# The last norm moved behind its transposes, and gates built for four tokens at a time

## The chip, the cores and the metric

The kernel runs on one core of one Trainium2 chip. The metric is the device time of one execution in microseconds (us). The shown runs of the kernel before took 3232.64, 3232.66 and 3237.02 us, the median is 3232.66 us. One more execution was recorded by the profiler; the profile below is of that one.

## The reference, cut to what matters

T = 256 tokens, width D = 2048, everything in fp32. Two blocks follow each other: attention and an MLP, then a recurrent mixer (HGRN2 and gated delta rule) and a layer of 16384 experts (PEER). The change touches the end of the mixer and the expert layer:

```
h  = h + mix @ w_out                                  # output projection, residual
hn = h * rsqrt(mean(h*h) + eps) * g                   # the norm ahead of the experts
q  = hn @ w_query                                     # 8 heads x 2 halves x 128
s1, s2 = q1 . sub_keys[0], q2 . sub_keys[1]           # 128 scores per half and head
v1, i1 = top_k(s1, 16); v2, i2 = top_k(s2, 16)        # then the best 16 of the 256 sums
expert = i1 * 128 + i2;  gate = softmax(best)
hid = gelu(hn @ u[e])                                 # kept where e is among the chosen
y   = sum over chosen e of gate_e * hid_e * v[e]
out = rmsnorm(h + y)
```

Chosen experts are not gathered. The kernel computes `hn @ u[e]` for all 16384 experts, multiplies the Gelu of it with a gate that is zero for experts not chosen, and multiplies the result with all of v.

## The kernel before, in words

**Products.** A weight matrix is read in pieces of 128 x 1024 (512 KB) into a tile `raw` by SP's DMA queue (line 90). ScalarE (ACT) rounds a piece to `hi` (L103), VectorE (DVE) forms the rest, `lo = raw - hi` (L104), and TensorE (PE) multiplies three times: hi with both parts of x, lo with x's first part. `wstat` (L117 to L128) holds the weights stationary: one call reads two pieces (the two halves of the contraction), runs 2 x 24 matmuls of 128 x 256 (L125) and gives 128 outputs for 256 tokens in a PSUM tile `acc`. For the expert layer there are 3 `raw`, 3 `hi` and 2 `lo` tiles. A piece's load waits on SP until its `raw` tile, used three pieces earlier, has been read by that piece's L104.

**End of the mixer.** `out_proj("w2_oa", [mixA], end_mix)` forms the last half of the output projection, 512 columns (`nb`, 0 to 3) and 128 tokens (`tt`, 0 and 1) at a time. `end_mix` adds each result to the residual x (L935), takes sums of squares on ACT, writes x to memory (`xd`), and after the last piece of a token half forms the norm's scale `r4` (a reduction and a small operation on DVE, a power on GpSimd, L247 and L248).

**The norm.** After that, x is scaled, `xs = x * r4` (L954, eight pieces of 128 x 512 on DVE). PE transposes xs in 32 pieces of 128 x 128 (L959); 16 times ACT and DVE split a transposed 128 x 256 piece into the two parts of `XT` (L114, L115). Then come the queries.

**Queries and scores.** 16 calls of `wstat` with `peer_q` give q, which ACT copies to `qT` (L1101). After each second call, eight fp32 matmuls with `sub_keys` (L1001) give the scores of a head, which ACT copies to `sc` (L1004). A generator, `topk`, works in the background on DVE from then on, into the first dozen u blocks, paced by the calls of `tick`.

**The u blocks.** 128 calls of `wstat` with `peer_u` follow. ACT applies Gelu to each result into a column block of `H` (L1150). Once the top-k is done, gates are built between the blocks by `gates` (L1104 to L1133), two tokens a call, 128 calls spread evenly up to block `G1` = 126: DVE compares a ramp with the first index of two tokens (`oh1`, L1108) and, for each token, with its second index times the gate (`oh2`, L1113), PE multiplies them (L1116), ACT copies one half of the result (L1120), DVE adds the other (L1123 or L1129) and multiplies into the columns of H that are there already (L1124, L1130, L1132); ACT copies the rest. Blocks that come after a token's gate get Gelu into `ut` (L1153) and a product on DVE (L1154).

**The v products** (L1180 to L1182) read H and end the kernel.

**What sets the order.** A scheduler arranges the instructions of the program into one list per engine; each engine takes its list strictly in order and waits on semaphores. Pieces under `tc.high_priority()` (loads, hi, lo, Gelu) are put as early as their inputs allow. Which tile an instruction may write is set by pools with a number of buffers (`bufs`).

## Time and profile before

| | |
|---|---|
| median of the runs shown | 3232.66 us |
| the profiled execution, and its span | 3235.04 us, 3233.3 us |
| TensorE busy | 3199.8 us, 99% of the span |
| VectorE busy | 2108.1 us, 65% |
| ScalarE busy | 1656.9 us, 51% |
| granted TensorE clock, mean | 0.997 of full speed |
| the norm ahead of the experts | about 1669 to 1686 us |
| queries; u blocks; v products | from 1686; from 1782; from 2516 us |
| top-k ends; gates | about 1840 us; 1883 to 2505 us |

The span is the time between the first and the last recorded instruction. A busy share is an average over the whole span: DVE is busy 90% of the time in some stages and far less in others. Rows of a timeline give the start and the duration of an instruction; an engine starts the next one a little before the last one's recorded end, so what an instruction costs in a row of instructions is the distance of starts. A matmul's recorded end is modelled; the distance of starts is what counts there too.

### The profile page before, as it was taken

How to read it: one execution, taken by the hardware profiler on the slowest of the kernel's cores; microseconds unless marked ns; L12 is line 12 of the kernel's file. 1: busy time of each engine (PE TensorE's matmuls, PEld its weight loads, DVE VectorE, ACT ScalarE, POOL GpSimd, SP SyncE). 2: the span in 40 equal slices, each digit the busy share in tenths (PEclk: the TensorE clock that was granted, in tenths of full speed). 3: DMA queues.
4: the chain of work that ended last, by engine and by line, in shares of the span. 5: the costliest groups of instructions: out<-in, count | busy, mean ns of one | idle time of the engine just before them, and what ended most of it. 6: DMA issues, size and time to landing. Idle time of an engine off the chain costs nothing.

```text
span 3233.3 us, 53579 instructions
## 1 busy us (share of the span) xinstructions
PE 3199.8 (99%) x21252; PEld 2909.6 (90%) x21252; DVE 2108.1 (65%) x3587; ACT 1656.9 (51%) x2453; POOL 25.2 (1%) x40
## 2 busy tenths in 40 slices
PE   9999999999999999999999999999999999999998
PEld 7989899899898889899889999999999888888886
DVE  4555665555555686478759867788888555555554
ACT  5447554444443564467444456655555544444444
POOL 0000000000000000000000000000000000000000
PEclk9999999999999999999999999999999999999999
DMA  6454555555555543354455555555555655555654
GB/s 226 151 169 160 186 189 195 193 191 190 190 189 194 185 138 114 111 164 141 151 182 177 177 177 184 185 184 184 184 181 185 209 190 193 191 191 192 215 190 162
DMA packets 162156, 578.71 MB, mean 179 GB/s; under 512 B 19056, under 2 KB 20720, under 8 KB 161520
## 3 DMA queue, kind: packets, MB, share of 16 engines
q1 hardware_dynamic: 156384, 565.36, 52.7%
q10 hardware_dynamic: 5520, 9.93, 0.9%
q8 instruction: 166, 2.72, 0.3%
q14 instruction: 86, 0.70, 0.1%
HBM read 571.02 MB, written 4.19 MB: 178 GB/s over the span
## 4 chain that ended last, share of the span: by engine, by line
PE 50%; DVE 2%; DMA 0%; ACT 0%; issue 0%; POOL 0%; DVEq 0%; POOLq 0%; ACTq 0%; SPq 0%
PE acc L125 23%; PE acc L1181 7%; PE acc L1180 7%; PE acc L1182 7%; PE acc L163 1%; PE acc L164 1%; PE acc L165 1%; PE misc L1116 1%; DVE lo L104 1%; PE misc L873 0%; DVE oh L1065 0%; DMA raw<-in_peer_v 0%; PE misc L1001 0%; ACT hi L103 0%; DVE es L1071 0%
## 5 line engine op out<-in xcount | busy, mean ns | idle before, releaser
L104 DVE TENSOR_TENSOR lo<-raw,hi 128x1024 fp32r<-128x1024 f32 x987 | 1206.6, 1223 | 854.5 <-ACT hi L103 497.4
L103 ACT ACTIVATE hi<-raw 128x1024 fp32r<-128x1024 f32 x1010 | 1071.0, 1061 | 1232.7 <-PE acc L164 359.4
L125 PE MATMUL acc<-xt,hi 128*128 128x256 f32 x8704 | 1522.8, 279 | 0.2 <-ACT hi L103 0.2
L125 PEld LDWEIGHTS acc<-xt,hi 128*128 128x128 f32 x8704 | 1321.4, 188 | 4.4 <-issue 3.2
L125 PE MATMUL acc<-xt,lo 128*128 128x256 f32 x4168 | 1159.0, 278 | 3.0 <-DVE lo L104 3.0
L125 PEld LDWEIGHTS acc<-xt,lo 128*128 128x128 f32 x4168 | 786.9, 189 | 4.2 <-DVE lo L104 4.2
L1181 PE MATMUL acc<-hi,xt 128*128 128x512 f32 x1024 | 402.7, 393 | 0.2 <-DVE xt L112 0.2
L1182 PE MATMUL acc<-lo,xt 128*128 128x512 f32 x1024 | 399.1, 390 | 1.6 <-DVE lo L104 1.6
L1180 PE MATMUL acc<-hi,xt 128*128 128x512 f32 x1024 | 400.3, 391 | 0.0
L1182 PEld LDWEIGHTS acc<-lo,xt 128*128 128x128 f32 x1024 | 192.2, 188 | 44.8 <-DVE lo L104 3.3
L1180 PEld LDWEIGHTS acc<-hi,xt 128*128 128x128 f32 x1024 | 192.2, 188 | 44.4 <-ACT hi L103 0.3
L1181 PEld LDWEIGHTS acc<-hi,xt 128*128 128x128 f32 x1024 | 192.4, 188 | 40.7 <-DVE xt L112 0.6
L164 PE MATMUL acc<-hi,act 128*128 128x512 f32 x512 | 199.5, 390 | 0.0
L165 PE MATMUL acc<-lo,act 128*128 128x512 f32 x512 | 199.5, 390 | 0.0
L163 PE MATMUL acc<-hi,act 128*128 128x512 f32 x512 | 199.2, 389 | 0.0
L163 PE MATMUL acc<-hi,xt 128*128 128x512 f32 x384 | 155.9, 406 | 2.1 <-ACT hi L103 2.1
L164 PE MATMUL acc<-hi,xt 128*128 128x512 f32 x384 | 151.4, 394 | 0.0
L165 PE MATMUL acc<-lo,xt 128*128 128x512 f32 x384 | 151.1, 394 | 0.0
L1113 DVE SCALAR_TENSOR_TENSOR oh<-c_iota,sl,slg 128x256 fp32r<-128x256 f32 x256 | 120.2, 477 | 0.0
L163 PEld LDWEIGHTS acc<-hi,act 128*128 128x128 f32 x512 | 96.1, 188 | 19.9
L164 PEld LDWEIGHTS acc<-hi,act 128*128 128x128 f32 x512 | 96.1, 188 | 19.9
L165 PEld LDWEIGHTS acc<-lo,act 128*128 128x128 f32 x512 | 96.1, 188 | 19.5
(580 smaller groups left out, 2874.9 us busy)
## 6 DMA issues: line engine op xcount, KB each, us to landing
raw<-in_peer_u SPq DMA_DIRECT2D x256, 512.0 KB, 3.6
raw<-in_peer_v SPq DMA_DIRECT2D x194, 512.0 KB, 4.3
raw<-in_w_up SPq DMA_DIRECT2D x128, 512.0 KB, 3.6
raw<-in_w_down SPq DMA_DIRECT2D x128, 512.0 KB, 3.5
raw<-in_w_qkf SPq DMA_DIRECT2D x32, 512.0 KB, 3.5
raw<-in_w_qka SPq DMA_DIRECT2D x32, 512.0 KB, 3.5
raw<-in_w_b SPq DMA_DIRECT2D x32, 512.0 KB, 3.5
raw<-in_w_fq SPq DMA_DIRECT2D x32, 512.0 KB, 3.9
```

Source lines behind the costliest of these rows:

```text
L103: S.activation(hi, r, AF.Copy)
L104: V.tensor_tensor(out=lo, in0=r, in1=hi.bitcast(F32), op=OP.subtract)
L125: PE.matmul(ps, lhsT=a[:, w], rhs=X[s][:, j, b], start=(s == 0 and j == 0 and a is hi and b == 0), stop=(s == 1 and j == 7 and a is lo))
L163: PE.matmul(ps, lhsT=x[:, 0], rhs=hi[:, w], start=(first and j == 0), stop=False)
L164: PE.matmul(ps, lhsT=x[:, 1], rhs=hi[:, w], start=False, stop=False)
L165: PE.matmul(ps, lhsT=x[:, 0], rhs=lo[:, w], start=False, stop=(last and j == 1))
L1113: V.scalar_tensor_tensor(oh2, iota[:, None].to_broadcast([128, 2, 128]), sl2[:, t:t + 1], slg.bitcast(F32)[:, t, :, None].to_broadcast([12 ...
L1116: PE.matmul(gps[:, j * 256:(j + 1) * 256], lhsT=oh1[:, j], rhs=oh2.rearrange("p a b -> p (a b)"), start=(j == 0), stop=True, skip_group_ch ...
L1180: PE.matmul(o, lhsT=x[:, 0], rhs=hi[:, w], start=first, stop=False)
L1181: PE.matmul(o, lhsT=x[:, 1], rhs=hi[:, w], start=False, stop=False)
L1182: PE.matmul(o, lhsT=x[:, 0], rhs=lo[:, w], start=False, stop=last)
```

## The change

**The norm.** x is transposed unscaled: r4 is one factor per token, and Gelu's argument, q and the scores are linear in x. `end_mix` now calls `xt_piece` (eight transposes, four splits with the gain `gcols`) as soon as columns `nb` of x are there (nb 0 to 2); the last eight transposes come in the background of the first query product, which runs on the old pools. `bcast` copies r4 along the free dimension into `r4B` (two diagonal matrices on DVE, two fp32 matmuls, an ACT copy). The scale is applied to the scores (two ACT copies with a scale per head in place of one) and to each u block: DVE forms `t = ps * r4B` (128 x 256) ahead of Gelu, which now reads `t` in SBUF. The 8 pieces of L954 are gone. mixA lies in two tiles of another pool.

**The gates.** A call of `gates` serves four tokens, 64 calls: `oh1` is one instruction of 128 x 512, `oh2` stays one per token, the sum and its copy stay one per two tokens, the products with H are one per H tile for four tokens. Buffers: `oh1` 2 to 1, `oh2` 4 to 3, `gs` 1 (it shared `ut`, 2), `ut` 2 to 1, `scr` 2 to 1.

```diff
     def end_mix(nb, tt, ps):
...
             rsqrt(r4[:, tt:tt + 1], s4[:, tt:tt + 1], 1, 1.0 / D)
-
-    out_proj("w2_oa", [mixA], end_mix)
+        elif tt == 1:
+            xt_piece(x, nb, XT, gcols[:, 4])
+
+    def end_norm():
+
+        with tc.high_priority():
+            xt_piece(x, 3, XT, gcols[:, 4])
+        yield
+        bcast(r4, r4B, xp)
+
+    out_proj("w2_oa", mixA, end_mix)
...
-    XT = new_xt()
-    nx = xq.enter_context(tc.tile_pool(name="nx", bufs=1, reuse_waits="tile"))
-    xs = [nx.tile([128, 2, 512], F32, name="xs", bufs=4) for _ in range(4)]
-    for tt in range(2):
-        for nb in range(4):
-            V.tensor_scalar(out=xs[nb][:, tt], in0=x[:, tt, nb * 512:(nb + 1) * 512], scalar1=r4[:, tt:tt + 1],
-                            scalar2=None, op0=OP.mult)
-    for c in range(16):
-        ps = misc()
-        for tt in range(2):
-            PE.transpose(ps[:, tt * 128:(tt + 1) * 128], xs[c // 4][:, tt, c % 4 * 128:(c % 4 + 1) * 128], ident)
...
+    bg.append(end_norm())
+    first_q = wstat(I["peer_q"][0], XT)
+    drain()
...
-        S.activation(sc, sps.rearrange("p (i n) -> p i n", i=4), AF.Copy)
+        for tt in range(2):
+            S.activation(sc.rearrange("p (a b) n -> p a b n", a=2)[:, :, tt],
+                         sps.rearrange("p (a b n) -> p a b n", a=2, b=2)[:, :, tt], AF.Copy, scale=r4[:, tt:tt + 1])
...
     def gates(g, c):
...
+        t0 = 4 * g
+        oh1 = pp2.tile([128, 4, 128], F32R, name="oh1", bufs=1)
+        V.tensor_tensor(out=oh1, in0=iota[:, None].to_broadcast([128, 4, 128]),
+                        in1=sl1[:, t0:t0 + 4, None].to_broadcast([128, 4, 128]), op=OP.is_equal)
+        gs = pp2.tile([128, 4, 128], F32, name="gs", bufs=1)
+        for i in range(2):
+            gps = misc()
+            for j in range(2):
+                t = t0 + 2 * i + j
+                oh2 = pp2.tile([128, 2, 128], F32R, name="oh2", bufs=3)
+                V.scalar_tensor_tensor(oh2, iota[:, None].to_broadcast([128, 2, 128]), sl2[:, t:t + 1],
...
+                PE.matmul(gps[:, j * 256:(j + 1) * 256], lhsT=oh1[:, 2 * i + j],
...
+            S.activation(gs[:, 2 * i:2 * i + 2], gv[:, :, 1], AF.Copy)
+            V.tensor_tensor(out=gs[:, 2 * i:2 * i + 2], in0=gv[:, :, 0], in1=gs[:, 2 * i:2 * i + 2], op=OP.add)
+        for i in range(2):
+            hv = H[i][:, :, t0:t0 + 4].rearrange("p b t -> p t b")
+            d = min(max(c - 64 * i, 0), 64)
             if d:
+                V.tensor_tensor(out=hv[:, :, :d], in0=gs[:, :, 64 * i:64 * i + d], in1=hv[:, :, :d], op=OP.mult)
+            if d < 64:
+                S.activation(hv[:, :, d:], gs[:, :, 64 * i + d:64 * i + 64], AF.Copy)
...
         with tc.high_priority():
+            t = pp2.tile([128, T], F32, name="ut", bufs=1)
+            V.tensor_tensor(out=t, in0=ps, in1=r4B, op=OP.mult)
             if n < T:
-                S.activation(hb[:, n:], ps[:, n:], AF.Gelu)
+                S.activation(hb[:, n:], t[:, n:], AF.Gelu)
             if n:
-                t = pp2.tile([128, T], F32, name="ut", bufs=2)
-                S.activation(t[:, :n], ps[:, :n], AF.Gelu)
+                S.activation(t[:, :n], t[:, :n], AF.Gelu)
                 V.tensor_tensor(out=hb[:, :n], in0=t[:, :n], in1=hb[:, :n], op=OP.mult)
-        while len(H) == 2 and done < 128 and b + 1 >= g0 + done * (G1 - g0) / 128:
+        while len(H) == 2 and done < 64 and b + 1 >= g0 + done * (G1 - g0) / 64:
```

The lines of the changed kernel are up to nine higher: the new product `t` is L1158, Gelu L1160 and L1162, the product with H of a block L1163; in `gates`, oh1 is L1119, oh2 L1127, the matmul L1130, the copy L1133, the sum L1134, the products with H L1139.

**Where instructions moved, first place: PE in the u blocks, around block 100.** In the kernel before, the two gate matmuls of a call stand behind the last matmul of one u block (`acc_25832`) and ahead of the first of the next (`acc_25912`):

```order
L125 MATMUL acc_25832<-xt_16306,lo_25842 128x256
L1116 MATMUL misc_25897<-oh2_25900,oh1_25898 128x256 [waits PE_49]
L1116 MATMUL misc_25897<-oh2_25903,oh1_25898 128x256
L125 MATMUL acc_25912<-xt_16305,hi_25915 128x256 [waits Activation_49]
L125 MATMUL acc_25912<-xt_16305,lo_25916 128x256 [waits DVE_49]
```

In the changed kernel three of the four gate matmuls stand there, between block 100 (`acc_25658`) and block 101 (`acc_25748`):

```order
L125 MATMUL acc_25658<-xt_15974,lo_25668 128x256
L1130 MATMUL misc_25727<-oh2_25728,oh1_25724 128x256 [waits PE_49]
L1130 MATMUL misc_25727<-oh2_25731,oh1_25724 128x256
L1130 MATMUL misc_25736<-oh2_25737,oh1_25724 128x256 [waits PE_49]
L125 MATMUL acc_25748<-xt_15973,hi_25751 128x256 [waits Activation_49]
...
L125 MATMUL acc_25748<-xt_15973,lo_25752 128x256
L1130 MATMUL misc_25736<-oh2_25740,oh1_25724 128x256 [waits DVE_49]
L125 MATMUL acc_25748<-xt_15973,hi_25751 128x256 x2
```

The fourth moved into the next block, behind 21 of its matmuls, and waits there for `oh2_25740` on DVE.

**Second place: DVE in the same stretch.** Before, with the block that ends (`ut_25814` is its Gelu), the sum and the two `oh2` of the next call, whose matmuls come a block later:

```order
L104 TENSOR_TENSOR lo_25842<-raw_25839,hi_25841 128x1024 [waits DMAHW5_49,PE_49,Activation_49]
L1108 TENSOR_TENSOR oh1_25978<-c_iota_16415,sl0_16417 128x256 [waits PE_49]
L1154 TENSOR_TENSOR H1_19031<-ut_25814,H1_19031 128x194 [waits Activation_49]
L1129 TENSOR_TENSOR ut_25826<-misc_25817,ut_25826 128x256 [waits Activation_49]
L1113 SCALAR_TENSOR_TENSOR oh2_25980<-c_iota_16415,sl1_16418,slg_16419 128x256
L1130 TENSOR_TENSOR H0_16414<-ut_25826,H0_16414 128x2x64 [waits DVE_49]
L1132 TENSOR_TENSOR H1_19031<-ut_25826,H1_19031 128x2x36
L1113 SCALAR_TENSOR_TENSOR oh2_25983<-c_iota_16415,sl1_16418,slg_16419 128x256
L104 TENSOR_TENSOR lo_25916<-raw_25913,hi_25915 128x1024 [waits DMAHW6_49,PE_49]
```

Now, from the end of block 100 (`ut_25719` is its scaled result) to the second piece of block 102:

```order
L1158 TENSOR_TENSOR ut_25719<-acc_25658,r4B_15972 128x256 [waits DVE_49,PE_49]
L104 TENSOR_TENSOR lo_25758<-raw_25755,hi_25757 128x1024 [waits DMAHW7_49,Activation_49]
L1163 TENSOR_TENSOR H1_19067<-ut_25719,H1_19067 128x196 [waits DVE_49,Activation_49]
L1134 TENSOR_TENSOR gs_25726<-misc_25727,gs_25726 128x256 [waits Activation_49]
L1127 SCALAR_TENSOR_TENSOR oh2_25740<-c_iota_16470,sl1_16473,slg_16474 128x256
...
L104 TENSOR_TENSOR lo_25818<-raw_25815,hi_25817 128x1024 [waits DMAHW0_49,PE_49]
L1134 TENSOR_TENSOR gs_25726<-misc_25736,gs_25726 128x256 [waits Activation_49]
L1119 TENSOR_TENSOR oh1_25880<-c_iota_16470,sl0_16472 128x512
L1139 TENSOR_TENSOR H0_16469<-gs_25726,H0_16469 128x4x64 [waits DVE_49]
L1139 TENSOR_TENSOR H1_19067<-gs_25726,H1_19067 128x4x37
L1158 TENSOR_TENSOR ut_25809<-acc_25748,r4B_15972 128x256 [waits PE_49]
L104 TENSOR_TENSOR lo_25824<-raw_25821,hi_25823 128x1024 [waits DMAHW1_49,Activation_49]
```

The call's last `oh2` stands behind the product with the finished block's Gelu and behind the sum; two more `oh2` of the next call stand where the dots are. On ACT, `hi_25817` (block 102) stands ahead of block 100's Gelu as the corresponding `hi` did before.

**Third place: ACT between the first and the second query product.** Before, the first piece of the second (`hi_16496`) stood ahead of the copy of the first result:

```order
L114 ACTIVATE xt_16306<-misc_16377,gcols_88 128x256 [waits PE_49]
L103 ACTIVATE hi_16496<-raw_16494 128x1024 [waits DMAHW6_49]
L114 ACTIVATE xt_16306<-misc_16382,gcols_88 128x256 [waits PE_49]
L103 ACTIVATE hi_16502<-raw_16500 128x1024 [waits DMAHW7_49,DVE_49,PE_49]
L1101 ACTIVATE qT_16491<-acc_16430 128x256 [waits PE_49]
L103 ACTIVATE hi_16559<-raw_16557 128x1024 [waits DMAHW0_49,DVE_49,Activation_49]
```

Now:

```order
L114 ACTIVATE xt_15974<-misc_16421,gcols_88 128x256 [waits PE_49]
L947 DMA xd_15969<-x_87 256x1x512
L1112 ACTIVATE qT_16485<-acc_16369 128x256 [waits PE_49]
L278 ACTIVATE r4B_15972<-misc_16450 128x256 [waits PE_49]
L103 ACTIVATE hi_16490<-raw_16488 128x1024 [waits DMAHW6_49]
```

The first piece of the second product (`hi_16490`) now stands behind the copy of the first result and behind the copy of `r4B`.

## Rows read from the trace of the kernel before

**Rows 1.** The page: busy time, share and count of each engine.

```profile
PE 3199.8 (99%) x21252; PEld 2909.6 (90%) x21252; DVE 2108.1 (65%) x3587; ACT 1656.9 (51%) x2453; POOL 25.2 (1%) x40
```

**Rows 2.** Waits of PE over the span: line, releaser, us, times, longest.

```profile
PE misc L959 <- DVE xs L954: 3.5, 2, 3.1
...
PE misc L873 <- DVE aT L877: 2.0, 1, 2.0
```

**Rows 3.** Timeline of PE around 1670: start, duration, idle before.

```profile
1669.18 0.39 PE L165 MATMUL acc<-lo,xt 128*128 128x512 f32 x1
...
1673.69 1.11 PE L959 MATMUL misc<-ident,xs 128*128 128x128 f32 x4 [3.08 <-DVE xs L954]
```

**Rows 4.** Timeline of ACT: the copy of the first query product.

```profile
1686.06 0.39 ACT L1101 ACTIVATE qT<-acc 128x256 f32<-128x256 f32 x1 [1.54 <-PE acc L125]
```

**Rows 5.** Windows: busy time (count) of each engine, PEclk the granted clock.

```profile
1465.00:1467.00 2.00, 2.00 (x12) 2.00 (x11) 0.42 (x4) 1.99 (x3) 0.00 (x0) 0.50 0.03 10
1670.00:1675.00 5.00, 1.73 (x8) 1.08 (x8) 3.84 (x11) 1.52 (x4) 0.56 (x1) 0.70 0.37 142
1820.00:1840.00 20.00, 18.08 (x147) 17.47 (x148) 19.93 (x28) 7.04 (x9) 0.00 (x0) 1.00 0.48 159
```

**Rows 6.** Timeline of PE: eight fp32 score matmuls.

```profile
1697.17 1.05 PE L1001 MATMUL misc<-sub_keys,qT 128*128 128x128 f32 x8
```

**Rows 7.** Lines by form: a product of PSUM with a broadcast scale on DVE.

```profile
L282 DVE TENSOR_TENSOR pad<-acc,r3B 128x256 f32<-128x256 f32 x16 | 6.8, 424 | 17.6 <-PE acc L125 17.6
```

**Rows 8.** Timeline of PE: gate matmuls, each behind the end of a u block.

```profile
2456.80 0.40 PE L1116 MATMUL misc<-oh,oh 128*128 128x256 f32 x2
...
2462.50 0.40 PE L1116 MATMUL misc<-oh,oh 128*128 128x256 f32 x2
...
2468.19 0.40 PE L1116 MATMUL misc<-oh,oh 128*128 128x256 f32 x2
```

**Rows 9.** Timeline of DVE in the same stretch.

```profile
2462.75 1.23 DVE L104 TENSOR_TENSOR lo<-raw,hi 128x1024 fp32r<-128x1024 f32 x1 [0.90 <-PE acc L125]
2463.89 0.42 DVE L1108 TENSOR_TENSOR oh<-c_iota,sl 128x256 fp32r<-128x256 f32 x1
2464.80 0.41 DVE L1154 TENSOR_TENSOR H<-ut,H 128x238 f32<-128x238 f32 x1 [0.49 <-ACT ut L1153]
2465.13 0.42 DVE L1129 TENSOR_TENSOR ut<-misc,ut 128x256 f32<-128x256 f32 x1
2465.46 0.47 DVE L1113 SCALAR_TENSOR_TENSOR oh<-c_iota,sl,slg 128x256 fp32r<-128x256 f32 x1
2465.86 0.46 DVE L1130 TENSOR_TENSOR H<-ut,H 128x128 f32<-128x128 f32 x1
2466.22 0.42 DVE L1132 TENSOR_TENSOR H<-ut,H 128x110 f32<-128x110 f32 x1
2466.54 0.48 DVE L1113 SCALAR_TENSOR_TENSOR oh<-c_iota,sl,slg 128x256 fp32r<-128x256 f32 x1
...
2469.92 0.40 DVE L1154 TENSOR_TENSOR H<-ut,H 128x240 f32<-128x240 f32 x1
```

**Rows 10.** Timeline of ACT in the same stretch.

```profile
2463.38 1.06 ACT L103 ACTIVATE hi<-raw 128x1024 fp32r<-128x1024 f32 x1 [0.95 <-DMA raw<-in_peer_u]
2464.34 0.17 ACT L1150 ACTIVATE H<-acc 128x18 f32<-128x18 f32 x1
2464.41 0.36 ACT L1153 ACTIVATE ut<-acc 128x238 f32<-128x238 f32 x1
```

**Rows 11.** Tile raw, 1885 to 2505: idle before its instructions; landing times.

```profile
  DMA raw<-in_peer_u: 41.9, 33
...
DMA to landing us min/median/max: 3.0/3.6/6.1
```

**Rows 12.** Lines by form of ACT, 2300 to 2310: SBUF and PSUM sources.

```profile
L1133 ACT ACTIVATE H<-ut 128x74 f32<-128x74 f32 x1 | 0.3, 341 | 0.5 <-DVE ut L1129 0.5
...
L1150 ACT ACTIVATE H<-acc 128x84 f32<-128x84 f32 x1 | 0.2, 222 | 0.0
```

More of the change, by code (lines that the diff above doesn't have):

```diff
@@ L919, in build, with mix_a @@
     proj_tok("w2_ag", zA, AF.Silu)
-    mixA = xtp.tile([128, 8, 2, T], F32R, name="xt", bufs=2)
+    mixA = []
+    def mix_a(i):
+        while not set(range(4 + 4 * i, 8 + 4 * i)) <= made:
+            yield
+        mixA.append(hp.tile([128, 4, 2, T], F32R, name="Z", bufs=3))
+        yield from head_norm_t(oA[i], mixA[i], lambda h: hg, hp, 0, 4,
+                               z=zA[:, :, i * 512:(i + 1) * 512].rearrange("p a (h d) -> p a h d", h=4))
     for i in range(2):
-        bg.append(head_norm_t(oA[i], mixA, lambda h: hg, hp, 4 * i, 4,
-                              z=zA[:, :, i * 512:(i + 1) * 512].rearrange("p a (h d) -> p a h d", h=4),
-                              ready=lambda i=i: set(range(4 + 4 * i, 8 + 4 * i)) <= made))
+        bg.append(mix_a(i))
     for nb in range(4):
@@ L930, in build @@
     r4 = sm.tile([128, 2], F32, name="r4")
+    r4B = sm.tile([128, T], F32, name="r4B")
+    XT = new_xt()
     def end_mix(nb, tt, ps):
@@ L1094, in build @@
     for c in range(16):
-        ps = wstat(I["peer_q"][c], XT)
+        ps = wstat(I["peer_q"][c], XT) if c else first_q
         if c and c % 2 == 0:
@@ L1104, in gates @@
     def gates(g, c):
-        gps = misc()
-        oh1 = pp2.tile([128, 2, 128], F32R, name="oh1", bufs=2)
-        V.tensor_tensor(out=oh1, in0=iota[:, None].to_broadcast([128, 2, 128]),
-                        in1=sl1[:, 2 * g:2 * g + 2, None].to_broadcast([128, 2, 128]), op=OP.is_equal)
-        for j in range(2):
-            t = 2 * g + j
-            oh2 = pp2.tile([128, 2, 128], F32R, name="oh2", bufs=4)
-            V.scalar_tensor_tensor(oh2, iota[:, None].to_broadcast([128, 2, 128]), sl2[:, t:t + 1],
-                                   slg.bitcast(F32)[:, t, :, None].to_broadcast([128, 2, 128]),
-                                   op0=OP.is_equal, op1=OP.mult)
-            PE.matmul(gps[:, j * 256:(j + 1) * 256], lhsT=oh1[:, j], rhs=oh2.rearrange("p a b -> p (a b)"),
-                      start=(j == 0), stop=True, skip_group_check=True)
```

29 lines of the change are left out of this document (9 added, 20 removed).

## The prediction, made before the changed kernel ran

> **What bounds the kernel now.** I read the page first: PE is busy 99% of the span, 3199.8 us [rows 1], so time is won or lost only where PE stands still, runs at the lower clock, or gets more to do. The change adds two small fp32 matmuls and takes none away. The list of PE's waits then says where it stands still: 3.5 us ahead of the norm's transposes, and little else near the change [rows 2]. Around the gates it waits almost nowhere. Two places remain to be worked out: the norm, where something can be won, and the u blocks, where PE has no wait yet and the change hangs one of its matmuls on DVE.
>
> **The norm, before.** The last matmul of the output projection starts at 1669.18 and gives way 0.23 later; the first query product is done when ACT copies it, at 1686.06, some 0.2 after PE's last matmul [rows 3, 4]. That is 16.45 us. The 48 matmuls in it are worth 48 x 0.114 = 5.5 us (two u blocks with four gate matmuls take 2468.19 - 2456.80 = 11.39, so 0.114 each [rows 8]). The 32 transposes are fp32 with 128 columns, as the score matmuls are, of which eight end within 1.05, so about 0.1 each [rows 6], 3.2 us. The rest, 7.8 us, is lost: 3.1 in one wait for xs [rows 3], some small ones, and the lower clock behind them (0.70 granted on average from 1670 to 1675, half speed for a good part of it [rows 5]).
>
> **The norm, after.** The 24 early transposes lie between matmuls of the output projection, and the last eight in the first query product, so the long wait goes. What is late next:
> - The add of the last 512 columns stands on DVE behind the first diagonal (which waits for GpSimd's power) and a `lo`, and PE reaches those transposes first: about 0.8, and 0.4 for the transposes of nb 2, which stand right behind their adds. 1.2 together, bounds 0.5 and 3.1 (the wait of before [rows 3]).
> - Between the first and second query product ACT now does the copy of q, then r4B, then the second product's `hi` (third place of the order). From PE's last matmul: 0.2, copy 0.36, r4B 0.36, hi 0.97 (2463.38 to 2464.34 [rows 10]), lo 1.22 [rows 9] are 3.1; two matmuls run ahead of the `lo` (0.2) and two score matmuls fill 0.2 that they would cost elsewhere: 2.7. The bounds are 1.5 (the copies are short and the load stands ready) and 5 (sub_keys, now issued later on the same queue, lands late).
> - Two diagonal matmuls, of which one lies in this gap: 0.1 to 0.2.
> - A PE wait of 2.0 us earlier in the kernel [rows 2] was followed by a stretch at half speed (1465 to 1467 [rows 5]). This gap is as long; I take 3 us of half speed, which cost 1.5, bounds 0 and 3.
> The gain is 7.8 - 1.2 - 2.7 - 0.1 - 1.5 = 2.3 us, bounds about -3 and +6.
>
> **The top-k stretch.** DVE is full there (19.93 of 20 us [rows 5]) and PE waits for it in places. Each u block now has `t` on DVE as well, 0.33 each (the form of L282, 0.424 long [rows 7], with the distance of starts that the equally long sum has, 2465.13 to 2465.46 [rows 9]). Eleven blocks make 3.7 at most. As `lo` stands ahead of top-k work where it can, a part of this delays the top-k and not PE: 1.5 taken, bounds 0 and 3.7.
>
> **The u blocks with gates.** Count DVE's work first. Per four tokens the changed gates save one start of `oh1` and little else (the products with H cost per element: 0.36 for 128 elements, 0.32 for 110 [rows 9], so 0.65 for 256), about 0.2 x 64 = 13 us over the stage; `t` adds 108 x 0.33 = 36. By its share that would still fit beside PE. What does not fit is the place of the fourth gate matmul (first and second place of the order). Let F be the end of a u block. PE runs three gate matmuls and 21 of the next block, and at F + 24 x 0.114 = F + 2.73 it meets a matmul that waits for an `oh2`. On DVE this `oh2` stands behind the product with the finished block's Gelu (L1154 before, L1163 now) and the sum of the gates. In the rows that product starts at F + 1.73 in one block (2468.19 to 2469.92) and at F + 2.30 in the block ahead, where ACT's `hi` had waited 0.95 for its load, and Gelu stands behind that `hi` [rows 8, 9, 10]. From there to the end of the `oh2` it is 2464.80 to 2465.46 plus 0.47 = 1.13 [rows 9]. So it is ready at F + 2.86 or F + 3.43, and PE waits 0.13 or 0.70. In the kernel before nothing of this touches PE: both `oh2` are made a block ahead. Everything of the u block is queued behind the waiting matmul, so the time is lost for good; waits under a us, 6 to 12 us apart, should not lower the clock.
>
> How often is the load late? Before, `hi` waits for a load 33 times, 41.9 us in all [rows 11], so it has no room to spare. And now there is a closed loop, with a group every second block, late in the stage. After the awaited `oh2`, DVE does two more `oh2` (0.80), a `lo` (1.14), a sum (0.33), `oh1` of 512 (0.60: 0.33 for 256 columns plus what a `lo` costs per column), H0 (0.65), H1 at 140 elements (0.38), `oh2` (0.40), `t` (0.33) and the `lo` that frees a `raw` tile (1.22): 5.85. Then the load, 3.65 with 0.1 for its issue and signal [rows 11], `hi` 0.96, Gelu 0.07 and 0.39 [rows 10], the product 0.33, the sum 0.33, the `oh2` 0.40: 6.23. That is 12.08 for two blocks, against 11.39 on PE: 0.69 lost per group. At the end of the stage H1 has 240 elements, 0.93. Early, without H1 and with half of H0, the loop is 11.3, and what is left is the direct wait of about 0.1; with H0 whole, 0.36. Over the blocks 18 (1883 less 1782 us, at 5.7) to 126, weighted by their number (18 at 0.1, 28 at 0.2, 62 at 0.67), that is 0.45 per group, and 64 x 0.45 = 29 us. (The groups come every 1.7 blocks, not every second; where two come in adjacent blocks, DVE's list without any idle time is some 6.8 us between the two `oh2`, against 5.9 on PE, so the loss is no smaller.) Bounds: nothing, if the `oh2` is ready in time; 64 x 0.13 = 8, if loads are never late; 64 x 1.0 = 64, if loads that overlap land 0.55 later than the median on average, which the longest, 6.1 [rows 11], leaves room for. I take 29: the loop rests on rows, and both ends need something that they don't show.
>
> The source of Gelu also changes, from PSUM to SBUF. A copy from SBUF of 74 columns (in strides) takes 0.341, Gelu from PSUM of 84 columns 0.222 [rows 12]; I leave it out of the sum. [...]
>
> **Switch to the v products.** The last gates end a block earlier, and the first `lo` of v comes 0.33 later; PE needs it after that: 0.
>
> **Sum.** Against the profiled execution, 3235.04 (span 3233.3, 1.7 around it): -2.3 + 1.5 + 29 = +28.2, 3263.2. That execution is 2.4 above the median of the runs: 3260.8, so 3261.
>
> **Rivals.**
> 1. The loads keep up, and only the direct wait is left: +8 in the gates, 3240. For it: a median landing of 3.6 and many blocks in which `hi` waited for PE instead. Against: `t` and the burst of four tokens put the `lo` that frees the tile later than before. Chance 0.13.
> 2. The loads overlap more and land later, 1.0 per group: 3235.04 - 2.3 + 1.5 + 64 - 2.4 = 3296. For it: DVE's two `lo` follow each other closer in the burst. Against: at a slower pace each load has more room. Chance 0.13.
> 3. The other side: the awaited `oh2` is ready, because Gelu starts before F + 1.0 and the product with it before F + 1.60. That is the point from which it decides; then the gates cost nothing, and -0.8 remains: 3231.8, no change. Against it: the earliest start in the rows is F + 1.73. Chance 0.07.
> 4. As 3, and the gap between the query products stays short enough to cost neither clock nor wait, and the top-k absorbs `t`: 7.8 - 1.2 - 0.1 = 6.5 gained, 3226, faster. Chance 0.05. That the change doesn't do what it says I exclude: the order shows the transposes among the projection's matmuls and half the calls of the gates.
>
> **How the numbers follow.** My forecast has 0.62, 3261, with its own range of 3248 to 3276 from 0.25 to 0.7 lost per group. Rival 1 lies inside the range that I give, 3238 to 3288; half of rival 2, rivals 3 and 4 are left out, 0.19. What can be told from no change here is 0.2%, 6.5 us: the forecast and rivals 1 and 2 are slower, 0.88, rival 3 is the same, 0.07, rival 4 faster, 0.05.
>
> **What would show it.** In the list of PE's waits, a line for the gate matmul (L1130) waiting for `oh2` (L1127), near 64 times and near 29 us, small at 1900 and near 0.7 to 0.9 a time at 2450; DVE less than full in between, ACT's `hi` waiting for loads more often than 33 times. At the norm: no wait over 1.5 us ahead of the transposes, one near 2.3 us between the first and the second query product, and a short stretch at the lower clock behind it. It is wrong if L1130 shows no waits, if the waits are on `lo` (L125) instead, or if the stage ahead of the experts moves by more than 6 us either way.

## The result, and the profile after

The changed kernel takes 3272.06 us (median of 5 runs, 3269.66 to 3276.97) against 3236.59 (5 runs) for the kernel before: a ratio of 1.0115, 95% interval 1.0100 to 1.0131, so 1.0 to 1.3% slower. (Beside the later experiments the kernel before had medians of 3232.9 to 3234.1 us, so the loss may be some 3 us larger than these two medians say.) The profiled execution has a span of 3270.2 us, 36.9 more than before. Where the time went, read off the two timelines (us):

| stretch | before | after | forecast of the difference |
|---|---|---|---|
| first add of the last projection to the last query copy (norm in it) | 135.2 | 131.9 | -2.3 |
| last query copy to the first gate matmul (top-k in it) | 108.7 | 107.5 | +1.5 |
| last query copy to the first v product (u blocks) | 738.6 | 778.9 | +30.5 with the top-k's 1.5 |
| first v product to the issue of the last store | 713.5 | 712.3 | 0 |

**Waits of PE.** This is the list of PE's waits of the changed kernel, in the form of [rows 2]:

```profile
PE misc L1130 <- DVE oh L1127: 19.3, 30, 1.9
...
PE misc L874 <- DVE aT L878: 2.0, 1, 2.0
...
PE misc L1010 <- ACT qT L1112: 0.3, 1, 0.3
```

The wait for xs is gone, and one that the kernel before did not have leads the list: the gate matmul, for `oh2`. The list counts only time in which PE is recorded idle, and a recorded matmul covers its modelled tail. By the distances of starts beyond 0.114 it is more: 30.4 us ahead of 69 gate matmuls, of which the fourth of a group 21.8 in 50 and the third 7.8 in 15, and 6.9 us, 0.1 each, ahead of 67 matmuls that follow a late one. Of the 64 groups, 19 stand in the block right after the block of the group before, the others two blocks behind it: all waits of the third matmul are in those 19, and 20.1 of the fourth's 21.8 us in the others.

The stretches of the table add up to 35.8; the rest lies ahead of them, where the first stretch starts anywhere from 1638.7 to 1643.5 us over all the runs.

**A group late in the stage.** PE, in the form of [rows 8]:

```profile
2441.44 0.52 PE L1130 MATMUL misc<-oh,oh 128*128 128x256 f32 x3
...
2444.96 0.39 PE L1130 MATMUL misc<-oh,oh 128*128 128x256 f32 x1 [0.60 <-DVE oh L1127]
2445.19 0.40 PE L125 MATMUL acc<-xt,hi 128*128 128x256 f32 x2
...
2448.27 0.40 PE L1130 MATMUL misc<-oh,oh 128*128 128x256 f32 x2
...
2449.60 0.35 PE L1130 MATMUL misc<-oh,oh 128*128 128x256 f32 x1 [0.69 <-DVE oh L1127]
```

DVE beside it, in the form of [rows 9]:

```profile
2441.64 0.42 DVE L1158 TENSOR_TENSOR ut<-acc,r4B 128x256 f32<-128x256 f32 x1 [1.50 <-PE acc L125]
2441.99 1.22 DVE L104 TENSOR_TENSOR lo<-raw,hi 128x1024 fp32r<-128x1024 f32 x1
2443.80 0.38 DVE L1163 TENSOR_TENSOR H<-ut,H 128x216 f32<-128x216 f32 x1 [0.60 <-ACT ut L1162]
2444.10 0.42 DVE L1134 TENSOR_TENSOR gs<-misc,gs 128x256 f32<-128x256 f32 x1
2444.43 1.27 DVE L1127 SCALAR_TENSOR_TENSOR oh<-c_iota,sl,slg 128x256 fp32r<-128x256 f32 x3
...
2448.99 0.47 DVE L1127 SCALAR_TENSOR_TENSOR oh<-c_iota,sl,slg 128x256 fp32r<-128x256 f32 x1
```

ACT, in the form of [rows 10]:

```profile
2442.30 1.06 ACT L103 ACTIVATE hi<-raw 128x1024 fp32r<-128x1024 f32 x1 [2.43 <-DMA raw<-in_peer_u]
...
2443.39 0.37 ACT L1162 ACTIVATE ut<-ut 128x216 f32<-128x216 f32 x1
```

The first block ends at 2441.44 (F, as in the prediction, is the end of a u block). `t` and the `lo` start soon after, but ACT's `hi` waits for its load until 2442.30, Gelu ends behind it, and the product with Gelu starts at 2443.80, F + 2.36. Then come the sum and the `oh2`, whose recorded end is 2444.91; the fourth matmul starts at 2444.96, F + 3.52, where it could have started at F + 2.73. The second group comes in the next block, and there it is the third matmul that waits (2449.60): its `oh2` stands at the end of DVE's list for the two groups, which ran without a gap from 2443.80 (the matmul's release is inferred; its `oh2` starts at 2448.99 and ends at 2449.46).

**The loads**, in the form of [rows 11]:

```profile
  DMA raw<-in_peer_u: 38.5, 17
...
DMA to landing us min/median/max: 3.1/3.5/5.5
```

`hi` waits for loads fewer times than before (17, not 33) but 2.3 us a time, not 1.3.

**The norm.** PE from the last matmul of the projection to the second query product, in the form of [rows 3]:

```profile
1674.20 0.39 PE L166 MATMUL acc<-lo,Z 128*128 128x512 f32 x1
...
1675.82 0.39 PE L125 MATMUL acc<-xt,hi 128*128 128x256 f32 x2
1676.30 0.89 PE L260 MATMUL misc<-ident,x 128*128 128x128 f32 x5
...
1681.25 0.38 PE L277 MATMUL misc<-diag,ones 128*128 128x128 f32 x2
1681.88 0.71 PE L1010 MATMUL misc<-sub_keys,qT 128*128 128x128 f32 x4 [0.25 <-ACT qT L1112]
1683.10 0.50 PE L125 MATMUL acc<-xt,hi 128*128 128x256 f32 x2 [0.50 <-ACT hi L103]
```

ACT and then DVE in the same stretch:

```profile
1681.44 0.38 ACT L1112 ACTIVATE qT<-acc 128x256 f32<-128x256 f32 x1 [2.93 <-PE acc L125]
1681.72 0.38 ACT L278 ACTIVATE r4B<-misc 128x256 f32<-128x256 f32 x1
1681.99 2.95 ACT L103 ACTIVATE hi<-raw 128x1024 fp32r<-128x1024 f32 x3
```

```profile
1683.08 1.23 DVE L104 TENSOR_TENSOR lo<-raw,hi 128x1024 fp32r<-128x1024 f32 x1 [3.77 <-ACT hi L103]
```

The transposes no longer wait long (0.48 from 1675.82 to 1676.30 at most). The first product is copied at 1681.44, and the second product's first `hi` starts only at 1681.99, behind the two copies; its `lo` ends at 1684.31. The windows, in the form of [rows 5], show no lower clock behind that gap:

```profile
1675.00:1680.00 5.00, 4.91 (x42) 4.57 (x41) 3.80 (x10) 2.18 (x6) 0.55 (x1) 1.00 1.00 385
1680.00:1685.00 5.00, 3.48 (x26) 2.90 (x25) 1.92 (x2) 3.49 (x5) 0.00 (x0) 1.00 0.11 40
1685.00:1690.00 5.00, 5.00 (x45) 5.00 (x44) 2.08 (x3) 1.06 (x1) 0.00 (x0) 1.00 0.83 256
```

### The profile page after: what moved, and what is told of

Its sections match the earlier page's. It is cut to its first block, busy times and chain, and to the rows that moved or that the text cites. A ratio compares the mean times of both kernels' runs of the same rounds, so it can differ in the third digit from the quotient of the medians.

```text
span 3270.2 us, 53518 instructions
## 1 busy us (share of the span) xinstructions
PE 3220.1 (98%) x21256; PEld 2917.6 (89%) x21256; DVE 2146.7 (66%) x3544; ACT 1662.2 (51%) x2370; POOL 25.2 (1%) x40
## 4 chain that ended last, share of the span: by engine, by line
PE 41%; DVE 7%; DMA 2%; issue 2%; ACT 1%; POOL 0%; DVEq 0%; ACTq 0%; POOLq 0%; SPq 0%
PE acc L125 15%; PE acc L1191 7%; PE acc L1190 7%; PE acc L1189 7%; DVE lo L104 2%; DMA raw<-in_peer_u 2%; PE acc L164 1%; PE acc L165 1%; PE acc L166 1%; PE misc L1130 1%; DVE oh L1127 1%; ACT hi L103 1%; DVE H L1139 1%; DVE gs L1134 1%; PE misc L874 0%
## 5 line engine op out<-in xcount | busy, mean ns | idle before, releaser
L1191 PE MATMUL acc<-lo,xt 128*128 128x512 f32 x1024 | 401.9, 393 | 0.7 <-DVE lo L104 0.7
L1190 PE MATMUL acc<-hi,xt 128*128 128x512 f32 x1024 | 402.1, 393 | 0.1
L1189 PE MATMUL acc<-hi,xt 128*128 128x512 f32 x1024 | 398.6, 389 | 0.0
L164 PE MATMUL acc<-hi,xt 128*128 128x512 f32 x320 | 130.7, 408 | 2.0 <-ACT hi L103 2.0
L166 PE MATMUL acc<-lo,xt 128*128 128x512 f32 x320 | 127.3, 398 | 0.0
L165 PE MATMUL acc<-hi,xt 128*128 128x512 f32 x320 | 126.3, 395 | 0.0
L1127 DVE SCALAR_TENSOR_TENSOR oh<-c_iota,sl,slg 128x256 fp32r<-128x256 f32 x256 | 114.7, 477 | 0.0
```

What stands on the lines that cost most here:

```text
L164: PE.matmul(ps, lhsT=x[:, 0], rhs=hi[:, w], start=(first and j == 0), stop=False)
L165: PE.matmul(ps, lhsT=x[:, 1], rhs=hi[:, w], start=False, stop=False)
L166: PE.matmul(ps, lhsT=x[:, 0], rhs=lo[:, w], start=False, stop=(last and j == 1))
L1127: V.scalar_tensor_tensor(oh2, iota[:, None].to_broadcast([128, 2, 128]), sl2[:, t:t + 1], slg.bitcast(F32)[:, t, :, None].to_broadcast([12 ...
L1189: PE.matmul(o, lhsT=x[:, 0], rhs=hi[:, w], start=first, stop=False)
L1190: PE.matmul(o, lhsT=x[:, 1], rhs=hi[:, w], start=False, stop=False)
```

## The experiments

The theory: groups of four with three `oh2` buffers put the fourth gate matmul into the next block, where it waits for an `oh2` late on DVE's list; `t`, ahead of the `lo` that frees a `raw` tile, makes loads, Gelu and with them that `oh2` later still. The rivals: A, the 36 us of `t` on DVE cost; B, groups of four cost alone; C, late loads are all of it; D, the four-token list costs wherever its matmuls stand. In the table "u" is the time from the last query copy to the first v product in the profiled execution, and the waits are distances of starts beyond 0.114, ahead of the third and of the fourth matmul of a group.

| run | ratio to before, interval | u | third | fourth |
|---|---|---|---|---|
| before | | 738.6 | | |
| changed | 1.0115 (1.0100 to 1.0131) | 778.9 | 7.8 | 21.8 |
| gates of two, norm kept | 1.0012 (1.0004 to 1.0021) | 743.3 | | |
| groups of four alone | 1.0082 (1.0068 to 1.0096) | 763.1 | 3.9 | 9.9 |
| changed, without t | 1.0067 (1.0049 to 1.0084) | 765.5 | 3.4 | 10.3 |
| changed, half the loads | 1.0060 (1.0043 to 1.0078) | 762.0 | 7.7 | 6.5 |
| groups of four alone, four oh2 buffers | 1.0040 (1.0026 to 1.0054) | 752.9 | 3.8 | 2.6 |
| changed, t in PSUM | 1.0154 (1.0138 to 1.0169) | 785.7 | 9.5 | 25.6 |
| changed, t in PSUM, four oh2 buffers | 1.0093 (1.0077 to 1.0108) | 770.6 | 6.2 | 2.4 |
| gates of two, copies on DVE | 1.0008 (0.9999 to 1.0017) | 745.6 | | |
| the same, t behind lo | 1.0003 (0.9994 to 1.0012) | 740.8 | | |
| changed, t behind lo | 1.0069 (1.0056 to 1.0083) | 764.2 | 10.0 | 7.2 |
| four alone, four buffers, every second block | 1.0017 (1.0008 to 1.0026) | 740.2 | 0 | 0 |
| changed, the fourth oh2 first on DVE | 1.0057 (1.0043 to 1.0071) | 761.3 | 3.1 | 0 |

**Gates of two tokens, the norm's part kept.**

```diff
-        t0 = 4 * g
-        oh1 = pp2.tile([128, 4, 128], F32R, name="oh1", bufs=1)
+        gps = misc()
+        oh1 = pp2.tile([128, 2, 128], F32R, name="oh1", bufs=2)
...
-        while len(H) == 2 and done < 64 and b + 1 >= g0 + done * (G1 - g0) / 64:
+        while len(H) == 2 and done < 128 and b + 1 >= g0 + done * (G1 - g0) / 128:
```

> The changed kernel with the gates of before: two tokens a call, their buffers as before; the norm's part, with the product t ahead of each Gelu, stays. Theory (a gate matmul in the next block waits for an oh2 that stands behind Gelu's product on DVE; it takes the groups of four and t together): the gate matmuls stand between blocks again, so their waits go. The norm's gain of 2.1 us stays, t leaves 0 to 7 us of small waits: 3234 to 3242. Rival A (t alone, 36 us more on DVE, is what costs): nearly as slow as the changed kernel, 3262 or more. Rival B (the groups of four alone cost it): 3234, 2 us faster than before.

3237.79 us, 4 us slower than the runs of before beside it, in the theory's range. PE's waits in this run:

```profile
PE acc L125 <- DVE lo L104: 4.8, 9, 0.8
...
PE misc L1127 <- DVE oh L1124: 0.4, 2, 0.2
```

The waits for `oh2` are all but gone (by the distances of starts 2.5 us are left, in 9), so the groups of four are needed for the loss, and `t` alone costs 4.7 us in the u blocks, about what the norm gains. The profiled execution was the shortest of the twelve, 3233.5 us; where the others lose the rest of the 4 us is not shown. Rival A falls.

**Groups of four alone**, on the kernel before.

```diff
-        gps = misc()
-        oh1 = pp2.tile([128, 2, 128], F32R, name="oh1", bufs=2)
+        t0 = 4 * g
+        oh1 = pp2.tile([128, 4, 128], F32R, name="oh1", bufs=1)
...
+                oh2 = pp2.tile([128, 2, 128], F32R, name="oh2", bufs=3)
```

> The kernel before with nothing changed but the gates: four tokens a call, with the buffers of the change; the norm is as before and Gelu reads PSUM. Theory: the fourth gate matmul waits here too, but DVE has no t, so the wait is near the direct one of 0.1 to 0.3 a group, 64 groups: 8 to 18 us slower than before, 3243 to 3254. Rival A (t alone): the time of before, 3236. Rival B (groups of four alone): 38 us more than before, 3274.

3260.53 us, 27 slower: more than I expected, and two thirds of the whole loss. A group in its trace, PE and then DVE:

```profile
2214.86 0.52 PE L1119 MATMUL misc<-oh,oh 128*128 128x256 f32 x3
...
2216.79 0.39 PE L1119 MATMUL misc<-oh,oh 128*128 128x256 f32 x1
```

```profile
2215.11 1.23 DVE L104 TENSOR_TENSOR lo<-raw,hi 128x1024 fp32r<-128x1024 f32 x1 [1.55 <-PE acc L125]
2216.25 0.48 DVE L1116 SCALAR_TENSOR_TENSOR oh<-c_iota,sl,slg 128x256 fp32r<-128x256 f32 x1
```

In this order the fourth matmul stands 12 matmuls into the block, at F + 1.73 if nothing holds it, and its `oh2` right behind a `lo`; in the changed kernel it stands later, at F + 2.73, and its `oh2` behind the product with Gelu. So this run gives the price of the groups, and not of that order. Its `oh2` takes a buffer that the group's first matmul (2214.86) frees, so it cannot be made ahead; it stands behind a `lo` on DVE and is ready at 2216.73, and the matmul starts at 2216.79, 0.2 late. The matmul behind it is 0.1 late too. That repeats in nearly every group: 9.9 us ahead of fourth matmuls, 3.9 ahead of third ones and 6.9 on the matmuls behind, 20.7 of the 24.5 us that the u blocks lose.

**The changed kernel without t.**

```diff
-            V.tensor_tensor(out=t, in0=ps, in1=r4B, op=OP.mult)
...
-                S.activation(hb[:, n:], t[:, n:], AF.Gelu)
+                S.activation(hb[:, n:], ps[:, n:], AF.Gelu)
...
```

> The changed kernel without the product t: Gelu reads PSUM, and the norm's scale is left out of the expert dot products. Theory: as the groups of four alone, less the norm's 2 us: 3241 to 3252, waits of the gate matmuls 8 to 18 us in all. Rival A: 3234. Rival B: 3270.

3256.76 us; u blocks and waits are those of the groups of four alone. So 40.3 us in the u blocks are 24.5 to 27 for the groups and 13 to 16 that `t` adds to them, three times what it costs with gates of two.

**Half the loads.**

```diff
             for s in range(2):
-                r = early.pop(0) if early else load(src, s)[0]
+                if half and s:
+                    r = half[-1]
+                else:
+                    r = early.pop(0) if early else load(src, s)[0]
```

> The changed kernel with half of the loads of peer_u left out: the second piece of each u block reads the tile that the first piece has loaded, so its product uses the first half of the weights twice. A tile is then free for a load a whole block earlier. Theory: the waits that follow a late load go (a half to two thirds of the loss), those in which DVE's list itself is too long between two groups stay: 10 to 20 us less than the changed kernel, 3252 to 3262. Rival C (the load that comes late is all of it): 3238 or less. If loads play no part: 3272.

3253.4 us, within the theory's range: 17 us of the u blocks' 40 go. ACT's `hi` waits for no load between 1885 and 2500, where the changed kernel loses 33.6 us in 15 such waits. PE and DVE have the same order of instructions as in the changed kernel, so this is the changed kernel with the loads in time. The line for the fourth and the third matmul, which was 19.3 us in 30 waits:

```profile
PE misc L1136 <- DVE oh L1133: 6.1, 11, 0.7
```

By the distances of starts the fourth matmul's waits fall from 21.8 to 6.5, 0.13 a time in 49 groups, the third's stay at 7.7, and the matmuls behind a late one still cost 6.7. Late loads account for about what `t` adds, and not for all of the loss: rival C falls.

**Four buffers for oh2**, on the kernel before with groups of four; Gelu of the gated columns goes back to PSUM to make room.

```diff
-                t = pp2.tile([128, T], F32, name="ut", bufs=1)
+                t = ps
...
-                oh2 = pp2.tile([128, 2, 128], F32R, name="oh2", bufs=3)
+                oh2 = pp2.tile([128, 2, 128], F32R, name="oh2", bufs=4)
```

> The kernel before with gates of four tokens, as the run with only the groups of four, but with four oh2 buffers instead of three (the room comes from ut: Gelu of the columns with a gate is written back to PSUM and multiplied from there). The order then has all four gate matmuls of most groups behind the end of a block, ahead of the next. Theory (three buffers hold the fourth oh2, and with it the fourth matmul, back until the next block, where it waits): the 0.3 us a group go, the time of before: 3232 to 3239. Rival D (groups of four cost by their longer list on DVE or by more matmuls at once, wherever they stand): as the run with the groups alone, 3255 or more.

3245.2 us: less than half of the loss goes with a fourth buffer in the u blocks (24.5 to 14.3), not all of it; between my theory and rival D. Groups two blocks apart show four matmuls without a wait, and where groups come in adjacent blocks they wait:

```profile
2234.36 0.64 PE L1119 MATMUL misc<-oh,oh 128*128 128x256 f32 x4
...
2240.29 1.10 PE L1119 MATMUL misc<-oh,oh 128*128 128x256 f32 x4
```

The first takes 0.64 from start to the modelled end, the second, in the block after the group before, 1.10. Writing Gelu back to PSUM has no control of its own on the kernel before; the next run does the same.

**The same, a group at every second block.**

```diff
-        while len(H) == 2 and done < 64 and b + 1 >= g0 + done * (G1 - g0) / 64:
+        while len(H) == 2 and done < 64 and b < 126 and b + 1 >= g0 + done * 2:
```

> The kernel before with gates of four tokens and four oh2 buffers, as that run, but a group at every second block exactly, so never in adjacent blocks; 55 of the 64 groups come, the gates of the last tokens are left out, and with them 36 matmuls, 4 us. Theory (what was left of the loss with four buffers sits in groups of adjacent blocks, whose oh2 are not ready): no waits of the gate matmuls, 3226 to 3234. Rival D (the four-token list on DVE by itself): waits as in that run, 3239 or more.

No gate matmul waits, which settles where the rest sat: in groups of adjacent blocks. (The 740.2 us of the u blocks hold a wait of 4.3 of the first v product for ACT and lack 36 matmuls, 4.1; without both it is 740.0, 1.4 above before.) Between 1885 and 2500 ACT's `hi` waits 59 times for a load, 112.2 us, the largest sum of all the runs: late loads cost next to nothing where no gate matmul stands behind them. The time, 3239.53 us, is above what I expected all the same, and at rival D's figure, though without its waits. The profiled execution is the longest of the ten, 3248.11 us; in it the v products take 10 us more, with a mean granted clock of 0.93 from 2500 to 2550, around that wait (1.00 there in the kernel before). That lies at the switch to v and not in the gates; I did not pursue it, and where the median execution loses is not shown.

**t in PSUM, and with four oh2 buffers**, on the changed kernel.

```diff
-            t = pp2.tile([128, T], F32, name="ut", bufs=1)
+            t = ps
```

> The changed kernel with the product t, and Gelu of the gated columns, written back to PSUM instead of ut; oh2 keeps three buffers. This is only the control for the next run: no matmul moves. Theory: 3266 to 3278, the waits as in the changed kernel. If the place of t matters by itself (a source in PSUM for Gelu): several us less.

> As the control, with four oh2 buffers. Theory: the fourth gate matmul stands at the end of a block, and the direct wait of 0.3 a group goes; what follows from late loads no longer meets a matmul in mid-block; waits stay where two groups come in adjacent blocks and DVE's list is longer than the block: 3238 to 3254. Rival C (late loads alone): they still delay the list, 3262 or more. Rival D: 3268.

The control is slower than the changed kernel and above its range, 3280.39 us. Of the 6.8 us that its u blocks take more, 3.0 are one wait of the first v product for ACT; the waits ahead of the third and the fourth gate matmul are 5.5 longer, and small pieces shorter. I have no run that says why. With the fourth buffer it is 3261.82, and the u blocks are 15.1 shorter than in the control. The fourth matmul's waits go (25.6 to 2.4), but the first of a group now waits 8.8 us in all and some `lo` come late: the place of the matmul was the cause of its wait, and part of the lateness finds the next instruction. My range was missed by 8 us, and 3262 was rival C's figure; what tells against C is the run with half of the loads, not this one.

**Copies on DVE**, with gates of two.

```diff
-        S.activation(b, ps[:, :T], AF.Copy)
+        copy(out=b, in_=ps[:, :T]) if copy else S.activation(b, ps[:, :T], AF.Copy)
...
-            S.activation(qT, ps, AF.Copy)
+            S.activation(qT, ps, AF.Copy) if c else V.tensor_copy(out=qT, in_=ps)
```

> The changed kernel with the gates of before (two tokens a call), and the copies of the first query product and of r4B on DVE instead of ACT, so that the second product's hi is no longer behind them. Theory of the norm's new gap (hi and lo one after the other behind the copies): PE starts the second product about 1.0 us earlier than in the run with gates of two tokens; the whole is 3231 to 3238, hardly to be told from before. If the gap is set by something else, a load or the scores: no earlier.

From the first add of the projection to the last query copy this takes 130.6 us against 131.7 with the copies on ACT: 1.1 earlier, as expected. The whole, 3235.78 us, can't be told from before.

**t behind lo**, with gates of two and on the changed kernel.

```diff
-        with tc.high_priority():
-            t = pp2.tile([128, T], F32, name="ut", bufs=1)
-            V.tensor_tensor(out=t, in0=ps, in1=r4B, op=OP.mult)
+        t = pp2.tile([128, T], F32, name="ut", bufs=1)
+        V.tensor_tensor(out=t, in0=ps, in1=r4B, op=OP.mult)
+        with tc.high_priority():
```

> As the run with gates of two tokens and the copies on DVE, but the product t without high priority, so that on DVE it stands behind the lo of the next block's second piece, not ahead of it. Theory (t ahead of that lo frees the raw tile later, and the load and Gelu behind it come late): the u blocks take what they took before, 739 to 741 us from the last query to the first v product against 743 to 746, and the norm's 4 us are left as a gain: 3226 to 3233, 1 to 6 us faster than before. Rival A (t costs by its time on DVE, wherever it stands): as the run with t ahead, 3 us slower than before.

> The changed kernel (groups of four, three oh2 buffers) with only t's priority taken away, so that it stands behind that lo. Theory: the part of the loss that follows from late loads (some 16 us) goes, the direct wait of the fourth matmul (some 24 us in all) stays or grows by the 0.3 that t itself now stands ahead of Gelu: 3253 to 3264. Rival A: 3272.

On the changed kernel, 3256.65 us, in the expected range: 14.7 of the u blocks' 40.3 go, and what is left, 25.6, is what the groups of four cost alone. The loads are not the reason: `hi` still waits for them 15 times, 25.2 us, between 1885 and 2500. The new order moved more than `t`. In this block of its DVE list the `lo`, `t`, the sum and the awaited `oh2` follow each other, with no product with Gelu ahead of the `oh2`:

```profile
2449.89 1.23 DVE L104 TENSOR_TENSOR lo<-raw,hi 128x1024 fp32r<-128x1024 f32 x1 [1.27 <-issue]
2451.04 0.42 DVE L1157 TENSOR_TENSOR ut<-acc,r4B 128x256 f32<-128x256 f32 x1
2451.37 0.42 DVE L1134 TENSOR_TENSOR gs<-misc,gs 128x256 f32<-128x256 f32 x1
2451.70 0.48 DVE L1127 SCALAR_TENSOR_TENSOR oh<-c_iota,sl,slg 128x256 fp32r<-128x256 f32 x1
```

So DVE does the same work, `t` included, at the price of the groups alone; but whether it is `t`'s place behind the `lo` or the `oh2`'s place ahead of the product that took the 14.7 off, this run does not tell. The next one was made for that. With gates of two the u blocks take 740.8 us, 2.2 above before, and the norm gains 4.4; the whole, 3233.7 against 3232.9 beside it (1.0003, 0.9994 to 1.0012), is just above the expected range and shows no gain that can be told. This is the best version found that keeps the norm's part, and it does not beat the kernel before.

**The fourth oh2 first on DVE**, on the changed kernel; `t` stays ahead of the `lo`.

```diff
-                V.scalar_tensor_tensor(oh2, iota[:, None].to_broadcast([128, 2, 128]), sl2[:, t:t + 1],
+                with tc.high_priority() if i and j else ExitStack():
+                    V.scalar_tensor_tensor(oh2, iota[:, None].to_broadcast([128, 2, 128]), sl2[:, t:t + 1],
...
```

> The changed kernel with one thing altered: the building of a group's fourth oh2 has high priority, so that on DVE it stands right behind t, ahead of the lo, of the product with the finished block's Gelu and of the sum; t stays ahead of the lo, and loads are as late as they were. The fourth matmul then stands 5 matmuls into the next block, at F + 0.9. Theory (a late load reaches PE only by way of Gelu, the product and the oh2 behind it): t ends near F + 0.5 and the oh2 near F + 1.05, so a wait of 0.1 to 0.25, and 0.1 behind it, in every group, none longer: u blocks of 752 to 764 us, the whole 3246 to 3258, while ACT's hi goes on waiting for loads. Rival C (late loads reach PE by another way, through lo): waits of PE on lo in their place, 3265 or more.

3252.06 us (3251.02 to 3253.96), as the theory expected: 17.6 of the 40.3 go, though loads are as late as ever (26 waits of `hi`, 49.5 us, between 1885 and 2500). A block of its trace in which the load is late, ACT, DVE and PE:

```profile
2425.87 1.06 ACT L103 ACTIVATE hi<-raw 128x1024 fp32r<-128x1024 f32 x1 [2.34 <-DMA raw<-in_peer_u]
...
2426.96 0.37 ACT L1163 ACTIVATE ut<-ut 128x216 f32<-128x216 f32 x1
```

```profile
2425.30 0.42 DVE L1159 TENSOR_TENSOR ut<-acc,r4B 128x256 f32<-128x256 f32 x1 [1.50 <-PE acc L125]
2425.64 0.48 DVE L1128 SCALAR_TENSOR_TENSOR oh<-c_iota,sl,slg 128x256 fp32r<-128x256 f32 x1
2426.04 1.22 DVE L104 TENSOR_TENSOR lo<-raw,hi 128x1024 fp32r<-128x1024 f32 x1
2427.36 0.38 DVE L1164 TENSOR_TENSOR H<-ut,H 128x216 f32<-128x216 f32 x1
```

```profile
2425.10 0.52 PE L1131 MATMUL misc<-oh,oh 128*128 128x256 f32 x3
...
2426.17 0.39 PE L1131 MATMUL misc<-oh,oh 128*128 128x256 f32 x1
```

ACT, Gelu and the product come as late as in the changed kernel (the product at F + 2.26, F being 2425.10), but the `oh2` stands ahead of the product and ends at 2426.12, and the fourth matmul starts 0.05 behind it, with no wait to speak of (it stands six matmuls into the block here). So in the changed kernel late loads reach PE through Gelu, its product and the `oh2` behind it. By the run with half the loads that way costs about 17 us. The u blocks here, 761.3, are as long as in that run (762.0), but of other parts: this order takes off the fourth matmul's direct wait and part of the third's too, and adds some on the first two matmuls and, in small part as rival C has it, 2.7 where PE waits for a `lo` (in the changed kernel, from the first gate on, nothing). A run of this order with half of the loads, which would show what late loads still cost in it, was not made. What stays, 22.7, is 9.0 ahead of the first three matmuls of a group, nearly all of it in the 19 groups of adjacent blocks, 7.4 on matmuls behind a late one (73, at 0.1), those 2.7, and small pieces.

## Why the prediction was right

The forecast was 3261 us, slower, in a range of 3238 to 3288; measured was 3272, with the mechanism it named. One term of the u blocks was left out and the norm's clock term did not come; in the groups of adjacent blocks the number came out near by another wait than the one worked out. Step by step:

- **The norm.** -2.3 forecast, -3.3 measured (135.2 to 131.9; the three other traces with the norm of before have 136.3 to 136.8, the seven others with the changed norm and copies on ACT 131.6 to 132.5, so 3 to 5 us). The wait of 3.1 went and the gap between the query products came, as worked out: from where PE's last matmul of the first gives way (1681.25) to the end of the `lo` it is 3.06, where 3.1 was forecast. The lower clock behind it did not come (granted 1.00 in all windows), so the 1.5 for it were wrong; PE still had the second diagonal and the scores in that gap, but whether they kept the clock up is not shown. The copies on DVE shorten it by 1.1, which shows the cause.
- **Top-k.** `t` moved its end by 7.4 us (63.5 to 70.9 after the last query copy) and PE by nothing: the first gate came no later. +1.5 was forecast.
- **The gates.** The place was right: PE's new wait is on the matmul and the `oh2` that were named, 69 times where about 64 were forecast. The size was 40 us in the u blocks, not 29. The waits ahead of gate matmuls were sized well, 30.4 us: in the 45 groups that stand two blocks behind the last one the fourth matmul waits 0.45 on average, as forecast. The direct wait in it, forecast at 0.13, is 0.13 in the run with half the loads, which has the same order. The term that was missing is the matmul behind a late one, 0.1 a time, 6.9 us, which I had not counted; the other 3 us or so are small pieces. With the loads in time the u blocks still lose 23 us, not the 8 that I gave for the direct wait alone: 6.5 are that wait, 7.7 the third matmuls of adjacent groups, 6.7 the matmuls behind. With groups of four alone, in another order, the wait is 0.2 a time; 0.056 of it are the time from the recorded end of an `oh2` to the start of the matmul that waited for it, the same in most groups of that run.
- **The loop through the load.** Right in kind: taking half of the loads out, or the awaited `oh2` ahead of the product with Gelu, takes 17 us off, with late loads in the second case and without in the first. The forecast had 21 us for it, 29 less the 8 of the direct wait. (Its second sum is a little off: the terms as they stand give 6.13, and 6.23 only with 0.1 more than the 3.65 of the load; the trace of before shows that 0.1: SP issues a load at 2464.01, 0.03 behind the end of the `lo` in [rows 9], and the `hi` at 2457.08 starts 0.08 behind the landing of its load.) It does not come as the steady 0.67 a group that I worked out: the fourth matmul waits near 0.2 a time around 1900, as forecast, but 0.1 to 2.1 behind 2200, most of it where `hi` has just waited 2 to 4 us for its load, and 0.46 on average from 2400 to 2500, where I had 0.7 to 0.9. The sign that I gave for it was wrong: `hi` waits for loads less often, not more often, but longer. A late load is no sign of a loss: the kernel before has twice as many, and the run with gates of two has 63 of them between 1885 and 2500, 82.0 us. Whether `t` makes the loads late by its place ahead of the `lo` or by its 0.33 us per block is not separated by any run and stays open.
- **Gelu from SBUF.** Left out of the sum. The trace agrees in kind with [rows 12]: 216 columns from SBUF take 0.37 (2443.39 in the rows of ACT above), while the larger 238 columns from PSUM took 0.36 [rows 10]. With equal columns the two traces show 0.346 from PSUM (L1153 before, 216 columns) and 0.370 from SBUF (L1162), and for the columns without a gate, 40 of them, 0.183 (L1150) and 0.228 (L1160). It is a few hundredths in a wait of half a microsecond.
- **Adjacent blocks.** I had them as "no smaller" within the same average. In size that holds, 10.3 us in 19 groups, 0.54 each. But it is a separate wait, mostly that of the third matmul, 7.8 us, it stays without late loads (7.7), and it is what is left of the loss with four buffers. That the forecast's average covered it is luck.
- **The rivals.** Rival 1 (only the direct wait, 3240) fell, as late loads cost 17 us; its price was low too, since the kernel with its loads in time takes 3253. Rivals 3 and 4 (no wait) fell by the waits; rival 2 (1.0 per group, 3296) was too much: 37.3 / 64 is 0.58.

## What to carry to other kernels

When work is grouped, ask which instruction of the group can't be prepared ahead, because a buffer is one short, and on which in-order engine its user then stands: here a fourth small matmul, 0.114 us of work, held up the engine that bounds the kernel 50 times. An addition to an engine that is not full is judged by who waits behind it, not by its share: the same `t` cost about 15 us where the awaited `oh2` stood behind `t`, Gelu and its product, and next to nothing where that `oh2` came ahead of the product. A load that comes late costs next to nothing as long as no matmul hangs on what stands behind it: the largest sum of waits for loads, 112.2 us, was in a run without any wait of a gate matmul. Saving starts on an engine that doesn't bound the kernel gained nothing here: the groups of four alone made it 27 us slower.

## What the runs showed of the hardware that was not expected

Behind a gate matmul that had waited, the next one started late as well: 67 times in the changed kernel the distance of starts is 0.19 to 0.23 and not 0.114 (2444.96 to 2445.19 in its timeline). Waits of 0.1 to 2.1 us on PE, every 6 to 12 us, left the granted clock at 1.00 throughout the u blocks of that kernel. With DVE writing its product back to the PSUM tile that it reads, and Gelu reading and writing there, the kernel took 8 us more than with the product in SBUF (3280.39 to 3272.06), with longer waits of the gate matmuls and 3.0 us in one wait at the switch to v; the cause is open.
